# A three-layer float32 network on one core: SBUF laid out anew, operands of the split products at multiples of 256 bytes

## The chip, the core and the metric

The kernel runs on one NeuronCore of one Trainium2 chip. The metric is device time in microseconds of one execution, median of three runs. All arithmetic is float32; the large products run on TensorE in its `float32r` form.

## What is computed

A sequence of 256 tokens with 2048 features passes a first block (16 meta tokens are put ahead, so 272 tokens) and then a second block of two layers. Cut to the parts that carry the work:

```
h = concat(meta, x)                                   # block 1, 272 tokens
z = rmsnorm(h) @ w_in                                 # -> u, q_a, kv_a, k_pe
y = concat(rmsnorm(s5_mixer(u)), rmsnorm(mla_mixer(q_a, kv_a, k_pe)))
h = h + y @ w_out
h = h + (silu(conv3(gate)) * val) @ w_down            # gate, val = rmsnorm(h) @ w_up, 5504 each
x = rmsnorm(h)[16:]
for l in range(2):                                    # block 2, 256 tokens
    proj  = rms_norm(x) @ w_in[l]                     # four mixers of four heads, 128 wide
    mixed = concat(nsa, stick_breaking, forgetting, differential) @ w_out[l]
    x = x + rms_norm(mixed)
    x = x + rms_norm((gelu(conv3(gate)) * conv3(val)) @ mlp_w_down[l])   # 5632 each
```

## The kernel before

**Tiling.** Activations lie feature-major: a chunk is a tile of 128 features (partitions) by 256, 258 or 272 tokens. Each weight matrix streams through once, in half units of 128x1024 float32 (512 KB), loaded by SP's queue into `wraw` (five slots, names `wr`). `split` (line 532) turns each half unit into two quarters of 128x512: ScalarE writes the high part `wh`, VectorE the rest `wl = wr - wh`. Eight quarters are held in the pools `wh` and `wl`; in the feed-forward stages seven more pairs, `wxh` and `wxl`, come from `spare` (line 594). Activations are split in the same way (`split_act`, line 708) into `xh`/`xl` (16 chunks, pool `xp`), `yh`/`yl` (mixer outputs, pool `yp`) and `hhh`/`hhl` (the hidden layer of the feed-forward, five slots each, `hsplit`, line 1243).

**The split products.** Each product of a weight tile and an activation chunk is three matmuls into one PSUM bank, in `mm3`:

```
nc.tensor.matmul(acc, wh, xh, start=start, ...)   # line 626
nc.tensor.matmul(acc, wl, xh, start=False, ...)   # line 627
nc.tensor.matmul(acc, wh, xl, ..., stop=stop)     # line 628
```

The weight is the stationary operand (128 columns, 512 bytes in each partition), the activation streams as the moving operand: 256 columns are 1024 bytes in each partition. There are 8700 such triples. In `m2` the roles are exchanged: 512 columns of weights stream over stationary activations.

**The stages, in order of time** (us from the span's start): block 1's input projection, S5 mixer, latent attention and output projection, up to 430; its up product, 430 to 930 (43 pairs of a gate tile of 258 columns and a value tile of 256); its down product, 930 to 1165; then for each layer of block 2 projections and mixers (1180 to 1580, 2402 to 2840), up product (1580 to 2135, 2840 to 3357) and down product (2135 to 2387, 3357 to 3600). The last 20 us finish the norm and write out.

**What sets the order.** The program emits instructions one by one; a rough model of engine clocks (`_Model`) decides when the side work of a mixer or of an evacuation is emitted between matmuls. Nothing is reordered later. Pools are a stack: what is opened first lies lowest.

**Where operands begin.** A 16384-byte scratch for DMA descriptors lies at address 0, then four constants of 32 bytes each, then the pool `keep` with the residual `X`, then `xp` at 35424 (138 times 256, plus 96). A chunk slot is 272 float32, 1088 bytes, so each slot moves the start by 64 modulo 256: `xh` begins at 96 or 224, `xl` at 160 or 32. `wh`, `wl` and `wr` all begin at 96 modulo 256, `wxh` and `wxl` at 224. `hhh` and `hhl` lie behind the feed-forward's own tiles: at 32 modulo 256 in block 1, at 224 in block 2; `yh` and `yl` at 224 in block 2. Block 1's up product reads the gate from column 0 of `xh[k]` and the value from column 2 (line 1195), that is 8 bytes further.

Of the kernel before, what the change touches and what calls it, by code (L numbers as in the profile page):

```python
# [20 lines left out]
F32 = mybir.dt.float32  # L21
F32R = mybir.dt.float32r
# [7 lines left out]
D = 2048  # L30
L = 272      # tokens of block 1: 16 meta + 256
LQ = 258     # tokens 14..271: the ones whose output or conv input is needed
S = 256
CB = 16      # column of the residual tile where the 256 tokens begin
NP1 = 43     # gate/value pairs of block 1
# [4 lines left out]
# ---------------------------------------------------------------- layout on the host  # L40
# [49 lines left out]
CMP_AT = [14, 16, 18, 20, 22, 24, 25, 27, 28, 30, 31, 33, 34, 36, 37, 39]  # first products of the compression behind these halves  # L90
A_SEQ = [0, 3, 1, 2]  # mixers in the order of their projections: A, D, B, C
# [75 lines left out]
def _s5_consts():  # L167
    """Steps counted from the middle; which group each half of the partitions holds; which pair a group is in."""
    iota = np.broadcast_to(np.arange(L // 2) - 68.0, (128, L // 2))
    half = np.zeros((128, 128))  # L170
    pair = np.zeros((128, 32))
    g = np.arange(64)
    for p in range(128):
        half[g[g % 2 == p // 64], p] = 1
    pair[g, g // 2] = 1
    return np.concatenate([iota, half, pair], 1).astype(np.float32)
# [105 lines left out]
# ---------------------------------------------------------------- the kernel  # L282
# [4 lines left out]
class _Model:  # L287
    """A rough account of when each engine is through with what it was given; it only decides the order of emission."""
# [17 lines left out]
    def run(self, clk, eng, outs, ins, cost, done=60.0):  # L306
        """Returns the engine's clock after an instruction."""
        for ap in ins:
            for k in self.keys(ap):
                w = self.wr.get(k)  # L310
                if w is not None:
                    clk = max(clk, w[0] + (0.0 if w[1] == eng else 100.0))
        ok = [k for ap in outs for k in self.keys(ap)]
        for k in ok:
            for d in (self.rd, self.wr):
                w = d.get(k)
                if w is not None and w[1] != eng:
                    clk = max(clk, w[0] + 60.0)
        clk += cost
        for ap in ins:  # L320
            for k in self.keys(ap):
                self.rd[k] = (clk, eng)
        for k in ok:
            self.wr[k] = (clk + done, eng)
        return clk


class _Pool:
    """A tile pool; notes which slot a tile is in."""
# [12 lines left out]
class _Engine:  # L342
    """Passes calls on to an engine and keeps its clock."""
# [45 lines left out]
class Kern:  # L389
# [3 lines left out]
    def __init__(self, ctx, tc, A, out, parts, taps):  # L393
# [33 lines left out]
        self.raws, self.ready = {}, deque()  # L427
        p = self.keep = self.pool("keep")
        self.X = p.tile([128, 16, L], F32, name="X")
        self.xp = self.pool("xp")  # L430
        self.xh, self.xl = [None] * 16, [None] * 16
# [4 lines left out]
        self.wraw = self.pool("wraw", self.NRAW)  # L436
        self.wh = self.pool("wh", self.NQ)
        self.wl = self.pool("wl", self.NQ)
# [11 lines left out]
    def slot(self, name, c, dt=F32R):  # L450
        """A tile of one feature chunk in the slot name + c; what held the slot before is done with."""
        pool = self.xp if name[0] == "x" else self.yp
        return pool.tile([128, L], dt, name="%s%d" % (name, c))

# [8 lines left out]
    # ---- pacing  # L463
# [30 lines left out]
    def after(self, *engines, extra=150):  # L494
        """Absolute virtual time at which the engines have done what they were given."""
        return max([e.clk for e in engines]) + extra - self.t
# [17 lines left out]
    # ---- the stream of weights: loaded ahead, each quarter of a unit split into two 12 bit parts  # L514
# [45 lines left out]
    def release(self):  # L560
        """The uses of the quarters handed out last are out."""
        for x in self.used:
            if x is None:
                self.nfree += 1
            elif self.cap > self.NQ:
                self.extra.append(x)
        self.used = []
# [26 lines left out]
    def spare(self, st, n):  # L594
        """Room for n more quarters, split before the engines are busy with what a product waits for."""
        p = self.pool("wx", 1, st)
        self.extra = [tuple(p.tile([128, 512], F32R, name="wx%s%d" % (x, i)) for x in "hl") for i in range(n)]
        self.cap = self.NQ + n

    def unspare(self):  # L600
        """No further quarter goes there."""
        self.extra, self.cap = [], self.NQ

    def staged(self, n, *stages):
        """Runs the stages over n items, each a step behind the one before it."""
# [6 lines left out]
    def lead_in(self, gen, ahead):  # L612
        """The pre() of a product whose operands gen makes; weights split before carry the first steps."""
# [30 lines left out]
    def s4(self, b, ks, xs, n, pre=None, start=True, stop=True):  # L644
        """Four column tiles, outer loop over the chunks ks of the contraction."""
# [23 lines left out]
    def pair(self, accs, nk, xs, pre=None, tail=0, evac=None):  # L669
        """Two column tiles; a quarter holds two chunks of the contraction. The last tail quarters are taken together,  # L670
        one column tile after the other."""
# [24 lines left out]
    def m2(self, b, xh, xl, f, pre=None):  # L696
        """Token-major product: two tiles of 128 tokens against f columns."""
# [9 lines left out]
    # ---- norms  # L707
# [17 lines left out]
    def sumsq(self, count, n, eng):  # L725
        """Squares of count chunks: sq(c, src) squares one, add(c) adds it up; the last two stay apart."""
# [15 lines left out]
    def evacuate(self, dst, ps, gain, c, sq):  # L742
        """dst = gain * ps and the squares of ps, these first where they are waited for."""
# [6 lines left out]
    def turnaround(self, gen):  # L750
        """Statistics that everything waits for; the engines split weights meanwhile."""
# [5 lines left out]
    def presum(self, acc, n, bank):  # L757
        """The part of stats that belongs to the first of accs."""
# [4 lines left out]
    def stats(self, accs, n, nfeat, bank, rB, r_tok=None, wait=(), lock=False, pre=0):  # L763
        """rB[p, token] = rsqrt(sum of accs over partitions / nfeat + eps), on all partitions; r_tok the same by token."""
# [23 lines left out]
    def now(self, gen):  # L788
        """Emits a generator to its end at once."""
# [11 lines left out]
    # ================================================================ block 1  # L801
    def block1(self):
# [37 lines left out]
        # ---- input projection; the S5 mixer runs beside it  # L840
# [168 lines left out]
        # ---- q and k/v of the attention from their low-rank parts  # L1009
# [59 lines left out]
        # ---- the gate of the S5 mixer  # L1069
# [53 lines left out]
        # ---- latent attention beside the output projection of the S5 half  # L1123
# [27 lines left out]
        # ---- output projection of the attention half  # L1151
        parts, sqx, addx = self.sumsq(16, LQ, G)

        def evx(acc, t):
# [9 lines left out]
            for a in range(2):  # L1164
# [3 lines left out]
                self.split_act(a_[:, :LQ], b_[:, :LQ], xc, gn["ffn"][:, c:c + 1])  # L1168
# [14 lines left out]
        # ---- feed-forward  # L1183
        wx = ExitStack()
        self.spare(wx, 7)
        ff = ExitStack()
        fp = self.pool("f1", 1, ff)
# [7 lines left out]
        xf = lambda k, a: (self.xh[k][:, 2 * a:LQ], self.xl[k][:, 2 * a:LQ])  # L1195
# [37 lines left out]
    def conv(self, pool, u, w, name):  # L1233
        """Three taps over a tile that begins two tokens early."""
# [8 lines left out]
    def hsplit(self, pool, hh, k):  # L1243
        a = pool.tile([128, S], F32R, name="hhh", bufs=5)
        b = pool.tile([128, S], F32R, name="hhl", bufs=5)
# [3 lines left out]
    def down(self, pool, hh, n, last, q=None):  # L1249
        """All but the last four chunks of the down product, into all eight banks; last: the bank pair used before."""  # L1250
# [33 lines left out]
    def s5(self, sp, sp2, s5p, cc, u, ys, gn, state):  # L1284
        """The S5 mixer, two tokens to a step: S = lam B u[2j] + B u[2j+1], H[j] = lam^2 H[j-1] + S, y[2j+1] = C H[j],
        y[2j] = C lam H[j-1] + C B u[2j]. Each complex recurrence is a real one in the frame that turns with its state."""
# [263 lines left out]
    def mla(self, sp, cc, qn, qpe, kn, kpe, vv, yh, yl, accb, gain):  # L1550
# [10 lines left out]
        # meta queries of all heads at once, other heads' keys masked  # L1561
# [78 lines left out]
    # ================================================================ block 2  # L1640
    def layer(self, l, upd, wx, last):
# [7 lines left out]
        # x_new per chunk, its parts for the projection and its squares  # L1649
# [66 lines left out]
        # tiles of a mixer, once they are there; uses of each that are still to come  # L1716
# [7 lines left out]
        # ---- mixer A  # L1724
# [101 lines left out]
        # ---- output projection  # L1826
# [65 lines left out]
        # ---- feed-forward  # L1892
# [8 lines left out]
        ff = ExitStack()  # L1901
        fp = self.pool("f2", 1, ff)
# [84 lines left out]
    def rope(self, dst, src, n, kind):  # L1987
        """dst = src * cos + (R src) * sin, two tiles at a time; dst may be src."""
# [16 lines left out]
    def lock(self):  # L2005
        """Bank 7, for the side generators of block 1."""
# [3 lines left out]
    def take(self, n, m=0):  # L2010
        """Banks and head buffers, all at once."""
# [10 lines left out]
    def gates(self, E, vsw):  # L2022
        """Gates of mixer A and the running log forget of mixer C, from the token-major columns."""
# [19 lines left out]
    def compress(self, E, aux, ready):  # L2043
        """Compressed keys and values of mixer A."""
# [44 lines left out]
    def probs(self, bank, q, k, z, sm, scale, mul=None, bias=None):  # L2089
        """Causal softmax of one head (both query tiles) into z: queries on partitions."""  # L2090
# [24 lines left out]
    def turn(self, bank, z, pt, mask=None):  # L2115
        """Transposes z into pt: keys on partitions, [keys 0 x queries 0..255 | keys 1 x queries 128..255]."""
# [141 lines left out]
    def mix_b(self, E, M, need):  # L2258
# [3 lines left out]
        def heads(hs):  # L2262
# [10 lines left out]
            # what each key leaves and takes; the product of what the later keys leave  # L2273
# [141 lines left out]
```

## Time and profile before

| | |
|---|---|
| median of three runs | 3621.8 us (3620.7 to 3624.3) |
| span of the profiled execution | 3619.8 us |
| TensorE matmul busy | 3498.2 us, 97% |
| TensorE weight load busy | 3371.0 us, 93% |
| VectorE busy | 2427.3 us, 67% |
| ScalarE busy | 1715.0 us, 47% |
| GpSimd busy | 501.6 us, 14% |
| HBM read | 610.7 MB, 169 GB/s over the span |

The span is the time from the first to the last instruction of one execution; 2.0 us lie between it and the median. A matmul's record lasts some 280 ns, but the next one starts long before it ends, so the cost of a matmul in a dense stretch is read from the distance between starts, or from how many there are in 100 us.

### The profile page before, as it was taken

The numbers are of one execution on the slowest core, as the hardware profiler recorded it, in microseconds if no ns is written. First come the engines' busy times: TensorE is split into PE (matmuls) and PEld (weight loads), VectorE is DVE, ScalarE is ACT, GpSimd is POOL, SyncE is SP. The second block draws the span as 40 slices with busy tenths as digits, with TensorE's granted clock in tenths as the row PEclk, the third lists the DMA queues.
The fourth block names the chain that finished last, engine by engine and source line by source line (L and its number), as shares of the span: only waits on it lengthen the run. The fifth ranks groups of instructions, "written<-read, shape, count | busy, mean of one in ns | idle before, by whom it ended". The sixth has DMA issues, their size and how long they took to land. (4 is left out here: it accounts for less than half of the span.)

```text
span 3619.8 us, 70825 instructions
## 1 busy us (share of the span) xinstructions
PE 3498.2 (97%) x27995; PEld 3371.0 (93%) x27995; DVE 2427.3 (67%) x4592; ACT 1715.0 (47%) x3441; POOL 501.6 (14%) x547
## 2 busy tenths in 40 slices
PE   7879999999999999999999999999999999999997
PEld 7767999999999889899999999988889899999997
DVE  7896766666656656467777775565655777777654
ACT  5445544444555544454444444455445544444544
POOL 6652300000002100021000000030000300000002
PEclk9889999999999999999999999999999999999999
DMA  5323555555654644455555555536445455555553
GB/s 177 104 82 101 168 182 187 186 179 180 201 193 152 224 161 158 154 167 183 187 186 188 184 186 185 185 136 221 146 146 192 131 187 187 187 186 186 185 185 122
DMA packets 175022, 618.55 MB, mean 171 GB/s; under 512 B 20224, under 2 KB 24464, under 8 KB 174432
## 3 DMA queue, kind: packets, MB, share of 16 engines
q1 hardware_dynamic: 173488, 612.55, 51.0%
q8 instruction: 219, 3.59, 0.4%
q0 software_dynamic: 336, 0.77, 0.1%
q14 instruction: 115, 0.94, 0.1%
q10 hardware_dynamic: 864, 0.70, 0.1%
HBM read 610.72 MB, written 2.10 MB: 169 GB/s over the span
## 5 line engine op out<-in xcount | busy, mean ns | idle before, releaser
L379 DVE TENSOR_TENSOR wl<-wr,wh 128x512 fp32r<-128x512 f32 (+1 forms) x2000 | 1374.5, 714 | 826.7 <-ACT wh L379 823.4
L379 ACT ACTIVATE wh<-wr 128x512 fp32r<-128x512 f32 (+1 forms) x2014 | 1195.3, 623 | 898.3 <-PE ps L628 678.6
L628 PE MATMUL ps<-xl,wh 128*128 128x256 f32 (+2 forms) x4980 | 1420.2, 285 | 2.4 <-DVE xl L379 2.4
L626 PE MATMUL ps<-xh,wh 128*128 128x256 f32 (+2 forms) x4876 | 1395.6, 286 | 13.1 <-ACT xh L379 7.9
L627 PE MATMUL ps<-xh,wl 128*128 128x256 f32 (+2 forms) x4876 | 1389.4, 285 | 8.9 <-DVE wl L379 8.8
L626 PEld LDWEIGHTS ps<-xh,wh 128*128 128x128 f32 x4876 | 934.3, 192 | 26.7 <-issue 8.5
L628 PEld LDWEIGHTS ps<-xl,wh 128*128 128x128 f32 x4980 | 950.5, 191 | 3.6 <-DVE xl L379 3.5
L627 PEld LDWEIGHTS ps<-xh,wl 128*128 128x128 f32 x4876 | 932.8, 191 | 14.6 <-DVE wl L379 12.7
L626 PE MATMUL ps<-hhh,wh 128*128 128x256 f32 x1820 | 509.0, 280 | 2.3 <-ACT y L379 1.5
L628 PE MATMUL ps<-hhl,wh 128*128 128x256 f32 x1820 | 509.0, 280 | 0.1
L627 PE MATMUL ps<-hhh,wl 128*128 128x256 f32 x1820 | 508.0, 279 | 0.0
L626 PEld LDWEIGHTS ps<-hhh,wh 128*128 128x128 f32 x1820 | 342.4, 188 | 2.7 <-ACT y L379 1.7
L628 PEld LDWEIGHTS ps<-hhl,wh 128*128 128x128 f32 x1820 | 342.2, 188 | 0.3 <-DVE hhl L379 0.3
L627 PEld LDWEIGHTS ps<-hhh,wl 128*128 128x128 f32 x1820 | 342.2, 188 | 0.0
L379 POOL TENSOR_TENSOR acc<-acc,sq 128x256 f32<-128x256 f32 (+1 forms) x137 | 119.1, 869 | 1163.2 <-ACT sq L379 1158.2
L626 PE MATMUL ps<-yh,wh 128*128 128x258 f32 (+2 forms) x696 | 202.4, 291 | 12.8 <-DVE xl L379 8.6
L379 POOL TENSOR_TENSOR hh<-cv,cv 128x256 f32<-128x256 f32 x88 | 84.8, 964 | 896.4 <-DVE cv L379 855.3
L628 PE MATMUL ps<-yl,wh 128*128 128x258 f32 (+2 forms) x696 | 199.2, 286 | 2.0 <-DVE yl L379 2.0
L627 PE MATMUL ps<-yh,wl 128*128 128x258 f32 (+2 forms) x696 | 198.5, 285 | 0.0
L379 DVE SCALAR_TENSOR_TENSOR cv<-pad,cw,cv 128x256 f32<-128x256 f32 x352 | 180.6, 513 | 13.1
L628 PE MATMUL ps<-xl,wxh 128*128 128x256 f32 x588 | 167.5, 285 | 1.1 <-DVE xl L379 1.1
L379 DVE TENSOR_TENSOR wxl<-wr,wxh 128x512 fp32r<-128x512 f32 x230 | 162.3, 709 | 1.9 <-ACT wxh L379 1.9
(444 smaller groups left out, 4383.3 us busy)
## 6 DMA issues: line engine op xcount, KB each, us to landing
wr<-in_w_dram SPq DMA_DIRECT2D x1105, 512.0 KB, 4.6
wr<-in_cmpw_dram SPq DMA_DIRECT2D x32, 512.0 KB, 5.0
wr<-in_w_dram SPq DMA_DIRECT2D x16, 272.0 KB, 4.3
c2t<-in_c_dram SPq DMA_DIRECT2D x2, 1472.0 KB, 9.1
bc<-in_bc_dram SPq DMA_DIRECT2D x8, 256.0 KB, 3.6
X<-in_hT_dram SPq DMA_DIRECT2D x3, 544.0 KB, 10.0
out_dram<-X SPq DMA_DIRECT2D x5, 256.0 KB, 2.2
s5e<-yh SPq DMA_DIRECT2D x64, 17.0 KB, 2.1
```

The costliest lines, as they stand in the source:

```text
L379: return f(out, *a, **kw)
L626: nc.tensor.matmul(acc, wh, xh, start=start, stop=False, skip_group_check=True)
L627: nc.tensor.matmul(acc, wl, xh, start=False, stop=False, skip_group_check=True)
L628: nc.tensor.matmul(acc, wh, xl, start=False, stop=stop, skip_group_check=True)
```

## The change

The same instructions on the same data; what moves is where tiles lie in SBUF. The built programs have equal lists of instructions on TensorE and VectorE, in equal order, and on the other engines too but for a handful of waits (GpSimd two more and SP one fewer, ScalarE two more), which follow from tiles lying over other tiles than before. The scratch for DMA descriptors falls from 16384 to 4096 bytes; `pad0` (128 bytes) brings the next pool to 4352, 17 times 256; `xp`, `wh`, `wl` and `wraw` now come first, `keep` with the residual after them; a chunk slot is 320 float32, 1280 bytes, of which 272 are used; `hhh` and `hhl` get a pool of their own right behind `wx`. All of `wh`, `wl`, `wxh`, `wxl`, `wr`, `xh`, `xl`, `yh`, `yl`, `hhh`, `hhl` then begin at 0 modulo 256. In block 1's up product the chunks are now written and read at columns 14 to 271 of their slots, as elsewhere in block 1, so that the gate's moving operand begins 56 bytes behind such a multiple and the value's 64 bytes. Comments and docstrings are dropped. The diff, cut to its core:

```diff
+XW = 320
...
+        self.pool("pad0").tile([128, 32], F32, name="pad0")
+        self.xp = self.pool("xp")
+        self.xh, self.xl = [None] * 16, [None] * 16
+        self.wh = self.pool("wh", self.NQ)
+        self.wl = self.pool("wl", self.NQ)
+        self.wraw = self.pool("wraw", self.NRAW)
+        self.pool("pad1").tile([128, 40], F32, name="pad1")
         p = self.keep = self.pool("keep")
         self.X = p.tile([128, 16, L], F32, name="X")
-        self.xp = self.pool("xp")
-        self.xh, self.xl = [None] * 16, [None] * 16
...
-        self.wraw = self.pool("wraw", self.NRAW)
-        self.wh = self.pool("wh", self.NQ)
-        self.wl = self.pool("wl", self.NQ)
...
-        return pool.tile([128, L], dt, name="%s%d" % (name, c))
+        return pool.tile([128, XW], dt, name="%s%d" % (name, c))[:, 0:L]
...
-                self.split_act(a_[:, :LQ], b_[:, :LQ], xc, gn["ffn"][:, c:c + 1])
+                self.split_act(a_[:, 14:L], b_[:, 14:L], xc, gn["ffn"][:, c:c + 1])
...
+        self.hx = self.pool("hx1", 5, ff)
         fp = self.pool("f1", 1, ff)
...
-        xf = lambda k, a: (self.xh[k][:, 2 * a:LQ], self.xl[k][:, 2 * a:LQ])
+        xf = lambda k, a: (self.xh[k][:, 14 + 2 * a:L], self.xl[k][:, 14 + 2 * a:L])
...
-        a = pool.tile([128, S], F32R, name="hhh", bufs=5)
-        b = pool.tile([128, S], F32R, name="hhl", bufs=5)
+        a = self.hx.tile([128, S], F32R, name="hhh")
+        b = self.hx.tile([128, S], F32R, name="hhl")
...
+        self.hx = self.pool("hx2", 5, ff)
         fp = self.pool("f2", 1, ff)
...
-    nc = _bacc.Bacc("TRN2", target_bir_lowering=False, num_devices=1)
+    nc = _bacc.Bacc("TRN2", target_bir_lowering=False, num_devices=1, dynamic_dma_scratch_size=4096)
```

## Rows read from the trace of the kernel before

**Rows 1.** The page's parts 1 and 2: busy us by engine; granted clock, 40 slices.

```profile
PE 3498.2 (97%) x27995; PEld 3371.0 (93%) x27995; DVE 2427.3 (67%) x4592; ACT 1715.0 (47%) x3441; POOL 501.6 (14%) x547
...
PEclk9889999999999999999999999999999999999999
```

**Rows 2.** The view of waits, PE alone: us in total, times, longest us.

```profile
PE ps L507 <- DVE s5ab L379: 21.3, 6, 6.7
PE ps L512 <- POOL rtok L379: 12.4, 9, 3.0
PE ps L626 <- ACT xh L379: 9.4, 3, 6.0
```

**Rows 3.** Windows of 100 us, PE: length, busy (matmuls), granted clock, DMA share, GB/s.

```profile
950.00:1050.00 100.00, 100.00 (x885) 1.00 0.59 195
2170.00:2270.00 100.00, 100.00 (x844) 1.00 0.58 184
...
3400.00:3500.00 100.00, 100.00 (x845) 1.00 0.57 185
...
1700.00:1800.00 100.00, 100.00 (x846) 1.00 0.58 189
...
600.00:700.00 100.00, 100.00 (x832) 1.00 0.56 188
```

**Rows 4.** Timeline, PE, down products of block 1 and layer 0: start us, us.

```profile
1000.16 0.28 PE L628 MATMUL ps<-hhl,wh 128*128 128x256 f32 x1
...
1001.86 0.28 PE L628 MATMUL ps<-hhl,wh 128*128 128x256 f32 x1
...
2200.08 0.28 PE L628 MATMUL ps<-hhl,wh 128*128 128x256 f32 x1
...
2201.86 0.28 PE L628 MATMUL ps<-hhl,wh 128*128 128x256 f32 x1
```

**Rows 5.** Window of tile wh alone: PE, PEld, DVE, ACT, POOL busy (count).

```profile
2170.00:2270.00 100.00, 64.93 (x341) 53.83 (x339) 29.17 (x43) 27.18 (x43) 0.00 (x0) 1.00 0.58 184
```

**Rows 6.** Timeline, PE, short products; then tile hb: ns min/median/max of one.

```profile
1304.30 1.96 PE L507 MATMUL ps<-kcT,q 128*128 128x16 f32 x16 [0.27 <-DVE kcT L379]
1306.11 0.37 PE L626 MATMUL ps<-xh,wh 128*128 128x256 f32 x1
...
2726.14 0.82 PE L512 MATMUL ps<-ident,hb 128*128 128x128 f32 x6
...
L512 PE MATMUL ps<-ident,hb x136: 270/272/329, 1246.1 to 2728.7; 128*128 128x128 f32 x136
```

**Rows 7.** Groups of instructions by form, PE: count, busy us, mean ns, idle before.

```profile
L628 PE MATMUL ps<-xl,wh 128*128 128x256 f32 x4052 | 1148.4, 283 | 2.4 <-DVE xl L379 2.4
...
L626 PE MATMUL ps<-yh,wh 128*128 128x258 f32 x352 | 104.3, 296 | 11.8 <-DVE xl L379 7.6 <-ACT yh L379 4.0 <-DVE kpe L379 0.3
...
L626 PE MATMUL ps<-wh,xh 128*128 128x512 f32 x192 | 81.8, 426 | 0.0
...
L637 PE MATMUL ps<-xl,wh 128*128 128x256 f32 x16 | 4.4, 426 | 0.1
```

**Rows 8.** Timeline, PE, 512 columns of weights moving, layer 0: start us, us.

```profile
1417.40 0.39 PE L626 MATMUL ps<-wh,xh 128*128 128x512 f32 x1
...
1420.17 0.39 PE L626 MATMUL ps<-wh,xh 128*128 128x512 f32 x1
```

**Rows 9.** Windows by stage: length, busy of PE, PEld, DVE, ACT, POOL, clock, DMA.

```profile
0.00:310.00 310.00, 247.91 (x1907) 223.32 (x1907) 262.48 (x509) 153.38 (x355) 177.64 (x181) 0.91 0.38 125
310.00:430.00 120.00, 120.00 (x874) 105.93 (x873) 85.78 (x208) 64.82 (x152) 35.84 (x42) 1.00 0.39 129
...
1580.00:2135.00 555.00, 547.53 (x4559) 545.52 (x4559) 424.08 (x773) 253.91 (x474) 69.57 (x78) 0.99 0.55 179
```

**Rows 10.** The page's part 5: VectorE's rest of a quarter, by destination.

```profile
L379 DVE TENSOR_TENSOR wl<-wr,wh 128x512 fp32r<-128x512 f32 (+1 forms) x2000 | 1374.5, 714 | 826.7 <-ACT wh L379 823.4
...
L379 DVE TENSOR_TENSOR wxl<-wr,wxh 128x512 fp32r<-128x512 f32 x230 | 162.3, 709 | 1.9 <-ACT wxh L379 1.9
```

## Prediction

> **What bounds the kernel now.** [...] Busy does not say whether TensorE is held up, so the view of waits comes next: its longest waits are 21.3, 12.4 and 9.4 us in total [rows 2]. So the matmuls' own pace sets the end, and the question is what one costs. In stretches of 100 us in which TensorE never stops, with the clock at 1.00, there are 885 matmuls in block 1's down product, 844 to 846 in block 2's up and down products, 832 in block 1's up product [rows 3]: 113.0, 118.2 to 118.5, and 120.2 ns each. [...] The starts show the same: fifteen matmuls take 1.70 us in the one down product and 1.78 us in the other [rows 4], 113 and 119 ns.
>
> These two down products run the same code on tiles of the same size; every weight quarter of the first begins at 96 modulo 256, and the moving operand `hhh`/`hhl` at 32 there and at 224 in block 2. Is it the weights' place? In the window of layer 0, `wh` takes part in only 341 of 844 matmuls [rows 5] (two of each triple read it, so some 510 of 844 use these slots, and 330 the `wx` slots at 224); in the last layer, where no `wx` exists, all weights lie at 96, and the pace is the same (845) [rows 3]. So the moving operand's start is worth some 5 ns of 118, and the weights' start less than half a ns.
>
> **The change, part by part.** *Nothing is added, removed or reordered* on TensorE and VectorE; no queue is passed. Only places change, so the sum is counts times a change of pace.
>
> *The new pace* is not in the trace: no float32r matmul begins at 0 modulo 256. Lower bound: what a chain of other matmuls shows as the least distance for a load of 128 columns. Six transposes take 0.82 us, the last one 0.272, so (0.82 − 0.272)/5 = 110 ns; sixteen products with 16 columns, whose streaming is short, leave 1306.11 − 1304.30 = 1.81 us, 113 ns each, some first-start delay included [rows 6]. With the 10 ns steps of these rows, 108 to 113. [...] Upper bound of the likely: 113, the best pace seen, since operands that begin at 224 or 96 show that being off can cost more, and 0 is nearer to a whole number of pieces than 32 is. Upper bound in earnest: 118.5, no gain. I take 110, the transposes' row, as it has the same 128-column weight load and a stream that keeps up with it.
>
> (a) 256 moving columns. By form there are 25 groups, 21,408 matmuls, of which [rows 7] gives the first and the last. Block 1's up and down products have 43 × 16 × 3 = 2064 each of these, leaving 17,280 at 118.5 ns: 17,280 × 8.5 = 146.9 us.
>
> (b) Block 1's down product: 2064 × (113 − 110) = 6.2 us.
>
> (c) Block 1's up product: 2064 gates of 258 columns and 2064 values of 256, at 120.2. Their new starts, 56 and 64, are no multiples of 256. The gate stays 8 bytes off a multiple of 16, as the value is now: I give it nothing. The value gets a first piece of 192 bytes up to the next multiple of 256; between 32 (224 bytes, 113) and 224 (32 bytes, 118.5) I take 115: 2064 × 5.2 = 10.7 us. Ends: 0 for both, or 110 for both, 42 us.
>
> (d) 258 columns of `yh`/`yl`: three forms of 352 [rows 7]. Those before 310 us stand where VectorE is busy 262.5 of 310 us and TensorE 247.9 [rows 9]: VectorE's chain sets that stretch, so I count nothing. From 310 to 430 TensorE is never idle [rows 9]; two thirds of 1056 there, times 9 ns: 6 us.
>
> [...]
>
> Together 146.9 + 6.2 + 10.7 + 6 + 6.9 = 176.7 us.
>
> [...]
>
> *What is late next.* TensorE covers all the splitting and side work; with a shorter stream that cover shrinks. In layer 0's up product VectorE has 424 us in 555 [rows 9], 76%; shortened by 8.5/118.5 the stage is 515 and VectorE 82%: it keeps up. ScalarE's and VectorE's instructions get no cheaper: a `wl` at 96 takes 714 ns and a `wxl` at 224 takes 709 [rows 10]. In the mixers' stages chains of short steps (scores, softmax, transposes) end in TensorE, and what the stream gains there partly turns into waits. I take a tenth back, 17.7 us; ends: nothing and a fifth.
>
> *The smaller scratch and the new waits* on GpSimd, SP and ScalarE stand at the few loads of constants between stages; TensorE waits for GpSimd 12.4 us in all [rows 2]. Between −1 and +3 us; I take 0.
>
> Net 176.7 − 17.7 = 159.0 us. The span of 3619.8 becomes 3461; with the 2.0 us between span and median, 3621.8 − 159 = **3463 us**.
>
> **The rivals.**
>
> *Only as good as the best pace seen.* If 113 is the weight load's pace and not the stream's, (a) is 17,280 × 5.5 = 95 us, (b) is 0, (c) some 10, (d) and (e) half, 6: 111, less a tenth, 100 us; 3522 us. For it: the 113 ns of the short products; against it: the 110 of the transposes.
>
> [...]
>
> *The shorter stream becomes waits.* If the mixers' chains and VectorE take back half instead of a tenth, 177/2 = 88 us remain: 3534 us. For it, VectorE's 76%; against it, that the up product shows no wait of TensorE among the longest [rows 2].
>
> *All starts alike: slower.* After the change moving operand, next weight load and the splits' reads and writes all begin at 0 modulo 256. If the memory serves neighbours of equal start one after another, the pace becomes that of the worst stage now, 120.2: 17,280 × 1.7 + 2064 × 7.2 = 44 us more, 3666 us. It decides as soon as the mean pace is over 118.5. Against it: in layer 0's down product, `hhh` at 224 with `wx` at 224 is such a pair of equal starts already, and its window has 844 matmuls against 845 without any [rows 3, 5]; `wr`, `wh` and `wl` too share their start today.
>
> **How the numbers follow.** Forecast (pace 108 to 112) 0.65; best pace seen 0.16; no gain 0.07; half turned into waits 0.06; slower 0.06. The low end: 109 ns (another 17,280 + 2064 at 1 ns, 19 us), block 1's up product in full (31 more), nothing given back (18): 159 + 68 = 227, 3395 us. The high end: 113.3 ns, nothing in block 1's up product, half of (d) and (e), a fifth given back: (90 + 6) × 0.8 = 77, 3545 us. The rivals at 3522 and 3534 lie inside; some 0.18 stays outside. A measurement of this kernel tells some 0.2% from no change. Faster by more: 0.65 + 0.16 + 0.06 and a little of the rest, 0.87; within: 0.07; slower: 0.06.
>
> **What would show it.** Right: windows of 100 us in block 2's up and down products with some 905 matmuls instead of 845, block 1's down product at the same pace as block 2's (not above it as now), the 512-column starts 218 to 222 ns apart, and waits of TensorE up by some tens of us at most. Block 1's up product tells whether 64 or 256 is the unit: 832 grows to about 850 if only the value gains, to 900 if a multiple of 64 is enough. Wrong: 845 again (lines of 16), 885 everywhere (a weight load's pace), a pace near 110 with waits of 80 us and more (side work), or fewer than 840.

## The result, and the profile after

The change made the kernel slower, by 0.7%, which is more than the runs of either kernel spread. Its median is 3646.8 us (3641.4 to 3649.3, four runs) against 3623.1 (3620.7 to 3625.0, four runs) for the kernel before, a ratio of 1.0069 [1.0054, 1.0083]. The forecast was 3463 us. The profiled execution's span is 3644.3 us, 24.5 more than before.

The page of the changed kernel: first the busy us of each engine and the granted clock in 40 slices, as [rows 1]; then, from its table of groups, TensorE's third product of a triple and VectorE's rest of a quarter, as [rows 10] (lines 626 to 628 are now 630 to 632, line 379 is 380).

```profile
PE 3525.1 (97%) x27995; PEld 3400.4 (93%) x27995; DVE 2429.3 (67%) x4592; ACT 1714.4 (47%) x3441; POOL 502.2 (14%) x547
...
PEclk9889999999999999999999999999999999999999
...
L380 DVE TENSOR_TENSOR wl<-wr,wh 128x512 fp32r<-128x512 f32 (+1 forms) x2000 | 1375.3, 715 | 850.8 <-ACT wh L380 848.1
...
L632 PE MATMUL ps<-xl,wh 128*128 128x256 f32 (+2 forms) x4980 | 1417.1, 285 | 2.3 <-DVE xl L380 2.3
```

The counts of instructions, the clock, VectorE (715 ns a quarter for 714 before) and ScalarE (busy 1714.4 us for 1715.0) are as they were. TensorE alone is busy 27 us longer. Its waits did not grow; the view of waits, TensorE only (us in total, times, longest us), as [rows 2]:

```profile
PE ps L511 <- DVE s5ab L380: 20.4, 6, 5.7
PE ps L516 <- POOL rtok L380: 11.5, 9, 2.4
PE ps L630 <- ACT xh L380: 9.3, 3, 5.0
```

So the time went into the matmuls' own pace. Windows of 100 us in which TensorE never stops (length, busy us, matmuls, granted clock, DMA share, GB/s): block 1's up and down products, then up and down of layer 0 and up and down of layer 1. The same five stretches as [rows 3] are among them:

```profile
600.00:700.00 100.00, 100.00 (x845) 1.00 0.57 190
950.00:1050.00 100.00, 100.00 (x835) 1.00 0.55 183
1700.00:1800.00 100.00, 100.00 (x836) 1.00 0.56 180
2170.00:2270.00 100.00, 100.00 (x836) 1.00 0.59 185
2900.00:3000.00 100.00, 100.00 (x835) 1.00 0.56 191
3400.00:3500.00 100.00, 100.00 (x836) 1.00 0.57 184
```

Block 1's down product fell from 885 to 835 and block 2 from 844-846 to 836; block 1's up product, the one stage that the new layout leaves unaligned, rose from 832 to 845. The timeline of TensorE in layer 0's down product (start us, duration us), as [rows 4]:

```profile
2200.11 0.28 PE L630 MATMUL ps<-hhh,wh 128*128 128x256 f32 x1
2200.23 0.28 PE L631 MATMUL ps<-hhh,wl 128*128 128x256 f32 x1
2200.35 0.28 PE L632 MATMUL ps<-hhl,wh 128*128 128x256 f32 x1
...
2200.83 0.28 PE L630 MATMUL ps<-hhh,wxh 128*128 128x256 f32 x1
...
2201.91 0.28 PE L630 MATMUL ps<-hhh,wxh 128*128 128x256 f32 x1
```

Fifteen matmuls take 2201.91 − 2200.11 = 1.80 us: 120.0 ns each, and every single distance is 0.12 us, with `wh` and with `wxh` alike. 1.70 us in block 1's down product and 1.78 in this one stood there before. It is not the splits running beside it that hold TensorE up: between 2180 and 2350 us the mean distance is 120.0 ns for the 316 matmuls beside which neither VectorE nor ScalarE is busy, and 120.0 for the 1101 beside which one of them or both are.

Adding up the distances from one matmul's start to the next over the whole span, by kind, shows where the 25 us come from (to some 0.5 us, as it depends on which distances count as gaps). Matmuls of 256 columns: 2534.9 to 2561.4 us (+26.5). In these, the 2064 of block 1's down product give +13.7 (113.3 to 120.0 ns each), block 1's 2064 up values −5.9 (120.9 to 118.0), and the other 17,280 +18.7 (118.7 to 119.8). Matmuls of 258 columns give −1.7, of 512 −1.7 (230.3 to 227.4 ns each), the fp32 products −0.6, the longer gaps +2.8.

### The profile page after: what moved, and what is told of

The parts are those of the page before. It is cut to its first block, busy times and chain, and to the rows that moved or that the text cites. A ratio compares the mean times of both kernels' runs of the same rounds, so it can differ in the third digit from the quotient of the medians.

```text
span 3644.3 us, 70827 instructions
## 1 busy us (share of the span) xinstructions
PE 3525.1 (97%) x27995; PEld 3400.4 (93%) x27995; DVE 2429.3 (67%) x4592; ACT 1714.4 (47%) x3441; POOL 502.2 (14%) x547
## 4 chain that ended last, share of the span: by engine, by line
PE 51%; DVE 1%; POOL 1%; issue 1%; ACT 0%; DMA 0%; POOLq 0%; ACTq 0%; DVEq 0%
PE ps L630 17%; PE ps L631 16%; PE ps L632 16%; PE ps L511 2%; POOL acc L380 0%; DVE X L380 0%; PE ps L516 0%; DVE hb L380 0%; DVE y L380 0%; DVE wl L380 0%; DMA wr<-in_cmpw_dram 0%; DVE xh L380 0%; DVE xl L380 0%; POOL X L380 0%; ACT hb L380 0%
## 5 line engine op out<-in xcount | busy, mean ns | idle before, releaser
L380 POOL TENSOR_TENSOR acc<-acc,sq 128x256 f32<-128x256 f32 (+1 forms) x137 | 119.2, 870 | 1182.3 <-ACT sq L380 1178.9
```

Source lines behind the costliest of these rows:

```text
L380: return f(out, *a, **kw)
```

## The experiments

Every kernel is the changed one with the edit shown, save `e8_scratch`, which starts from the kernel before. "Triple" is the time of the three matmuls of a split product. Starts are always modulo 256 bytes, and "32 on 96" is a moving operand that begins at 32 with weights that begin at 96. Offsets in the diffs count elements of four bytes.

**All combinations at once.** Block 2's chunks get moving starts at every multiple of 16, and the weight slots starts at every multiple of 32.

```diff
+        o = 4 * c if self.shift and name[0] == "x" else 0
+        return pool.tile([128, XW], dt, name="%s%d" % (name, c))[:, o:min(o + L, XW)]
...
+            o = 8 * (self.nq % 8)
+            self.nq += 1
+            h = self.wh.tile([128, 576], F32R, name="wh")[:, o:o + 512]
+            l = self.wl.tile([128, 576], F32R, name="wl")[:, o:o + 512]
```

> The changed kernel with many starts at once. In block 2 the chunk k of xh and xl (k from 0 to 15) begins 16k bytes behind a multiple of 256, and the weight slots of wh and wl begin, in rotation, at 0, 32, 64 ... 224; wx stays at 0. Block 1 is as in the changed kernel. Theory M (the moving operand's start alone sets the pace): the distance of starts depends on k and not on the weight slot: 120 ns at k = 0, 113 at k = 2 (32 bytes), 118.5 at k = 14 (224 bytes). Theory C (moving operand and weights clash where their starts are equal): 120 ns for those pairs of chunk and slot whose starts agree modulo 256, and less, down to 113, for the others, at every k. [...]

One run took 3613.9 us against 3622.9 of the kernel before. The table takes block 2's runs of at least 12 successive matmuls with one pair of starts, called blocks here (the distances from the trace, the starts from the addresses in the built program). It leaves out a block's first two distances and its last, and gives the mean distance by the *difference*, moving start less weights' start, modulo 256:

```
difference  ns (blocks)      difference  ns (blocks)
   0       119.6 (138)         128      119.0  (95)
  16       114.6  (50)         144      118.6  (54)
  32       117.2  (96)         160      118.0  (93)
  48       118.2  (48)         176      119.3  (59)
  64       116.2  (87)         192      114.9 (100)
  80       119.1  (59)         208      119.0  (56)
  96       119.7 (100)         224      118.2  (96)
 112       117.5  (49)         240      117.1  (54)
```

Neither start alone explains this. With the moving operand at 0, weights at 0, 32, 64, 96, 128, 160, 192 and 224 give 119.6, 118.3, 116.3, 117.2, 119.7, 119.4, 116.1 and 117.7 ns. The difference does better: 0 on 0, 64 on 64 and 160 on 160 give 119.6, 119.5 and 119.3; 0 on 32, 96 on 128 and 224 on 0, all 224 apart, give 118.3, 118.1 and 118.3. Equal starts are nearly the worst, and starts 96 or 176 apart are as slow.

The differences 16, 64 and 192 have two paces each, and a block has one or the other: 192 runs at 113.6 in 65 blocks and at 117.5 in 35. Which one depends on what ran just before: all 28 blocks of 192 behind a chunk of difference 224 were slow, all 12 behind one of difference 0 were fast (28 of 28 and 11 of 12 in the finer map below). The 12, and 20 of the 28, are the same tile at the same pair of starts, `hhh` at 0 on 64. So something lasts beside the difference, perhaps how the two reads last fell into step; no row shows what it is.

**The same in steps of 4 bytes.**

```diff
-        o = 4 * c if self.shift and name[0] == "x" else 0
+        o = c if self.shift and name[0] == "x" else 0
```

> The map again with chunk k of xh and xl in block 2 beginning 4k bytes behind a multiple of 256 (k from 0 to 15), weight slots at 0, 32 ... 224 in rotation as in the first map, so that every multiple of 4 bytes appears as a difference. Theory C (the pace follows the difference of the two starts modulo 256): differences that both maps hold (0, 16, 32, 48 and their sums with 32) show the first map's paces (119.6 at 0, 114.6 at 16, 117.2 at 32, 114.9 at 192), whatever the two starts are alone. Theory M (the moving start alone): the pace goes by k. [...]

3620.4 us against 3623.2. At multiples of 16 most of the first map comes back (0: 119.6, 96: 119.5, 128: 119.6). The differences with two paces keep the paces and not the mean: 192 has 116.1, again from 113.4 and 117.8, and 64 has 117.7 for 116.2, as 65 of its 66 blocks run at the slower one. All weights begin at multiples of 32 here, so the rest modulo 16 is the moving operand's: starts at 0, 4, 8 and 12 past a multiple of 16 average 118.3, 120.5, 120.0 and 117.1 ns (586, 207, 219 and 222 blocks). No pair's mean in either pace lies below 113.3. So the place within 16 bytes matters too, by some 2 ns, though not as off or on a multiple alone: 12 past it is the quickest. The table within multiples of 16 has a spread of 5.

**One difference at a time.** `e2_w96` moves only the weights to 96, `e3_m32` only the moving operands to 32, `e4_m32_w96` both, which gives block 2's up products and layer 1's down product the pair that block 1's down product had in the kernel before.

```diff
+        self.pool("padw").tile([128, 24], F32, name="padw")
         self.wh = self.pool("wh", self.NQ)
...
-        self.pool("pad1").tile([128, 40], F32, name="pad1")
+        self.pool("pad1").tile([128, 16], F32, name="pad1")
...
+        p.tile([128, 24], F32, name="padx")
         self.extra = [tuple(p.tile([128, 512], F32R, name="wx%s%d" % (x, i)) for x in "hl") for i in range(n)]
```

> The changed kernel with the weights alone moved: wh, wl and wx begin at 96 modulo 256 instead of 0, the moving operands of the up products stay at 0. In the down products of block 1 and layer 0 the hidden layer slips to 96 as well, in layer 1 it stays at 0. Theory M: the up products of block 2 keep 833 matmuls in 100 us (120 ns); about 3647 us. Theory C: with unequal starts they rise to 850 to 885, the two down products with 96 on 96 stay at 833, layer 1's down product rises; 3560 to 3620 us.

```diff
-        return pool.tile([128, XW], dt, name="%s%d" % (name, c))[:, 0:L]
+        return pool.tile([128, XW], dt, name="%s%d" % (name, c))[:, 8:8 + L]
...
-        a = self.hx.tile([128, S], F32R, name="hhh")
+        a = self.hx.tile([128, XW], F32R, name="hhh")[:, 8:8 + S]
```

(and `hhl` like `hhh`).

> The changed kernel with the moving operands alone moved: xh, xl, hhh, hhl (and block 1's yh, yl) begin at 32 modulo 256, all weights stay at 0. Theory M: the pace of block 1's down product before, 113 ns, 885 matmuls in 100 us, in block 2's up products and in all down products; some 19,000 matmuls at 6.7 ns less: 127 us, 3520 us. Theory C: some pace below 120 as the starts differ, but 113 only by chance; 3520 to 3620 us.

> The changed kernel with both moved to the pair of block 1's down product before: moving operands at 32, weights at 96 modulo 256; in the down products of block 1 and layer 0 the hidden layer slips to 128. Theory M and theory C alike: 885 matmuls in 100 us in block 2's up products and in layer 1's down product, as that pair had before; 3520 to 3560 us. Where 128 on 96 comes out tells more: theory M says whatever the map shows for 128, theory C the pace that the map shows for a difference of 32. If neither pace appears, something else than these two starts set the 113 ns.

Against 3622.9 us of the kernel before: `e2_w96` 3621.8 (ratio 1.0001 [0.9989, 1.0013]), `e3_m32` 3599.1 (0.9932 [0.9916, 0.9949]), `e4_m32_w96` 3578.9 (0.9876 [0.9829, 0.9923]). Windows of `e2_w96`, TensorE, columns as above: block 1's down product, where `hhh` begins at 96 on 96, then the up products of layers 0 and 1, where the chunks begin at 0 on 96:

```profile
950.00:1050.00 100.00, 100.00 (x836) 1.00 0.56 182
1700.00:1800.00 100.00, 100.00 (x845) 1.00 0.56 181
...
2900.00:3000.00 100.00, 100.00 (x854) 1.00 0.52 178
```

Equal starts at 96 are as slow as equal starts at 0, 836 (a triple of exactly 360 ns), so a multiple of 256 has nothing to do with it; 0 on 96, difference 160, is 845 in one layer and 854 in the other. The weights' start, which the prediction priced at less than half a ns, is worth 9 to 18 matmuls in 100 us (the changed kernel has 836 and 835 there), and moving the weights alone takes back the 25 us that the change had lost. Windows of `e3_m32`, block 1's down and layer 1's up product:

```profile
950.00:1050.00 100.00, 100.00 (x859) 1.00 0.56 189
...
2900.00:3000.00 100.00, 100.00 (x852) 1.00 0.52 177
```

32 on 0 gives a triple of 350 ns in one stage and 353 in the other. Windows of `e4_m32_w96`, block 1's down product, then up and down of layer 0 and up of layer 1:

```profile
950.00:1050.00 100.00, 100.00 (x851) 1.00 0.55 185
1700.00:1800.00 100.00, 100.00 (x885) 1.00 0.61 202
2170.00:2270.00 100.00, 100.00 (x859) 1.00 0.59 189
2900.00:3000.00 100.00, 100.00 (x851) 1.00 0.53 181
```

Both up products run 32 on 96, difference 192; one is at the best pace seen, 340 ns a triple, the other at 353, and the four runs spread over 45 us around a median above the 3520 to 3560 us expected. So the two paces of one pair last for whole stages. In the two down products the hidden layer lies at 128 on 96 (in layer 0 for nine matmuls in ten): difference 32, and the triples take 353 and 350 ns, the two paces of 32 on 0 in `e3_m32`. That is the difference at work with both starts changed.

**Is it the load's length?** The second and third product load and compute 32 of the 128 weight columns.

```diff
+        m = min(32, acc.shape[0])
-        nc.tensor.matmul(acc, wl, xh, start=False, stop=False, skip_group_check=True)
-        nc.tensor.matmul(acc, wh, xl, start=False, stop=stop, skip_group_check=True)
+        nc.tensor.matmul(acc[:m], wl[:, :m], xh, start=False, stop=False, skip_group_check=True)
+        nc.tensor.matmul(acc[:m], wh[:, :m], xl, start=False, stop=stop, skip_group_check=True)
```

> The changed kernel with the second and third matmul of each triple cut to 32 of the 128 weight columns (so they add only to 32 rows of the output; the rest of the low parts is left out). The moving operands are read as before from 0 modulo 256, in full. A matmul streams while the weights of the next are loaded: the first and the second matmul of a triple then stream beside a load of 32 columns, the third beside one of 128. Theory C (the two reads disturb each other): the first two distances of a triple fall from 120 to about 108, the third stays between 113 and 120; 330 to 345 ns a triple instead of 360, some 890 matmuls in 100 us. Theory M (the moving read alone is slow from 0): all three stay at 120, 833 in 100 us.

3586.9 us, one run, against 3623.2. Groups by form, weight loads of the down products (count, busy us, mean ns), then the windows of layer 0's up and layer 1's down product:

```profile
L630 PEld LDWEIGHTS ps<-hhh,wh 128*128 128x128 f32 x1820 | 341.6, 188 | 19.3 <-ACT y L380 1.8 <-DVE X L380 1.1
L632 PEld LDWEIGHTS ps<-hhh,wl 128*32 128x32 f32 x1820 | 199.1, 109 | 0.0
```

```profile
1700.00:1800.00 100.00, 100.00 (x859) 1.00 0.59 193
...
3400.00:3500.00 100.00, 100.00 (x851) 1.00 0.56 188
```

A short load lasts 109 ns for the 188 of a full one, and the mean distance at difference 0 went from 120.0 ns to some 116.7 in block 1's down product and layer 0, and to 117.7 in layer 1. It did so in all three matmuls of a triple alike, within 1 ns, not in the two that stream beside a short load. So the pace of the stream depends on the loads around it, and theory M is out; that the load's reads hold up the stream's fits this but is not shown, as the cut matmuls also write fewer rows, and why the long load's neighbour gains as much as the others is open.

**Sixteen bytes apart.** Moving operands at 16, weights at 0.

```diff
+        return pool.tile([128, XW], dt, name="%s%d" % (name, c))[:, 4:4 + L]
...
+        a = self.hx.tile([128, XW], F32R, name="hhh")[:, 4:4 + S]
...
+        yh, yl = (yp.tile([128, 12 * S + 64], F32R, name=n)[:, 4:4 + 12 * S].rearrange("p (c n) -> p c n", c=12) for n in ("yh2", "yl2"))
```

> The changed kernel with every moving activation 16 bytes behind a multiple of 256 (xh, xl, yh, yl, hhh, hhl) and every weight at such a multiple. In block 1's up product gate and value then begin at 72 and 80. Theory C with the first map (16: 113.3 ns in 36 of 50 places): 885 matmuls in 100 us in block 2's up and down products and in block 1's down product; 3647 less some 20,000 times 6.5 ns, so about 3515 to 3535 us, and steadier over the rounds than the pair 32 on 96. Theory M: the pace of k = 1 in the first map, 118; 3610 us.

3591.0 us, ratio 0.9913 [0.9891, 0.9935]. Windows: block 1's down, layer 0's down and layer 1's down product:

```profile
950.00:1050.00 100.00, 100.00 (x885) 1.00 0.56 195
...
2170.00:2270.00 100.00, 100.00 (x845) 1.00 0.56 186
...
3400.00:3500.00 100.00, 100.00 (x860) 1.00 0.56 188
```

The same code with the same starts has three paces here: triples of some 340, 355 and 350 ns. The expectation, 885 in all of these stages and 3515 to 3535 us, was missed: the difference alone does not tell the pace.

**The scratch alone**, in the kernel before:

```diff
-    nc = _bacc.Bacc("TRN2", target_bir_lowering=False, num_devices=1)
+    nc = _bacc.Bacc("TRN2", target_bir_lowering=False, num_devices=1, dynamic_dma_scratch_size=4096)
```

> The kernel before with one part of the change alone: the scratch for DMA descriptors is 4096 instead of 16384 bytes; all else moves down by 12288 bytes, 48 times 256, so all starts modulo 256 stay. Theories C and M alike: no change, 3619 to 3626 us. If the smaller scratch held up loads, some us more.

3621.7 us, ratio 0.9996 [0.9986, 1.0005]: it costs and brings nothing.

**The best difference everywhere, and a push into the 340 ns pace.** Moving operands at 192, weights at 0; in `e9_kick` chunk 0 and every eleventh `hhh`/`hhl` begin at 0, because blocks of difference 192 behind one of difference 0 were fast. `e10_d192` is the same without these.

```diff
+        o = 0 if c == 0 and name[0] == "x" and self.xo == 48 else self.xo
+        return pool.tile([128, XW], dt, name="%s%d" % (name, c))[:, o:o + L]
...
+        o = 48 if self.nh % 11 else 0
+        self.nh += 1
+        a = self.hx.tile([128, XW], F32R, name="hhh")[:, o:o + S]
...
+        yh, yl = (yp.tile([128, 12 * S + 64], F32R, name=n)[:, 48:48 + 12 * S].rearrange("p (c n) -> p c n", c=12) for n in ("yh2", "yl2"))
```

(`self.xo` is 48 elements, 192 bytes, and 32 while block 1's up chunks are written.)

> Theory C with states: the pace of a pair of starts depends on their difference and on how the two reads fell into step; 192 has a state of 113.3 and one of 117.8 ns, which lasts, and the first map shows which one is entered: behind a chunk of difference 0 the fast one (20 of 21 in both maps), behind one of 224 the slow one. The changed kernel with moving activations at 192 and weights at 0, but the chunk 0 of xh and xl and every eleventh chunk of the hidden layer at 0, so that the step is set anew at the price of one chunk at 120. In block 1's up product gate and value begin at 184 and 192. Expected: 880 matmuls in 100 us in all up and down products of block 2 and in block 1's down product, some 860 in block 1's up product; 3647 - 102 - 13 - 9 = about 3523 us, within 10 us from run to run. Without states (the difference alone decides): a mean of the two, 115 to 116, 3560 us.

> The same without the chunks at 0: every moving activation at 192, all weights at 0. Theory C with states: whole stages at 113.3 and others at 117.8, by chance, so times that differ by tens of us from run to run, like the pair 32 on 96 (3555 to 3600 us). Without states: one pace everywhere, and times as close to each other as those of the kernel before.

`e9_kick` took 3537.1 us (3535.5 to 3540.1, four runs), ratio 0.9765 [0.9753, 0.9778], 14 us more than expected; `e10_d192` 3536.7 (3524.5 to 3560.3, six runs), ratio 0.9781 [0.9752, 0.981], mostly quicker than expected. Both beat both kernels by more than 80 us. Windows of `e9_kick`, all six stages:

```profile
600.00:700.00 100.00, 100.00 (x843) 1.00 0.56 185
950.00:1050.00 100.00, 100.00 (x879) 1.00 0.57 191
1700.00:1800.00 100.00, 100.00 (x882) 1.00 0.57 189
2170.00:2270.00 100.00, 100.00 (x882) 1.00 0.59 193
2900.00:3000.00 100.00, 100.00 (x881) 1.00 0.53 182
3400.00:3500.00 100.00, 98.52 (x864) 1.00 0.58 185
```

Its chunks at 192 have a median triple of 340 ns in every stage of block 2 and in block 1's down product, those at 0 354 to 360. Without the push the profiled run has 884 or 885 in these stages where TensorE never stops, but the runs differ by 36 us instead of 5. Four and six runs are few; that the push holds the 340 ns pace is likely by this, and not settled. It costs what it gains: the medians are equal. Block 1's up product (gate at 184, value at 192) stays at 843, where 860 was expected: its gates take a mean of 364.5 ns a triple, and the values behind them 348.8 in place of 340.

**What is 113.3 the pace of?** From `e10_d192`, once with short loads (the edit of `e6_short_load`) and once with short streams, where the second and third matmul of a triple stream 192 of 256 columns beside full loads:

```diff
+        c = n * 3 // 8 * 2
-        nc.tensor.matmul(acc, wl, xh, start=False, stop=False, skip_group_check=True)
-        nc.tensor.matmul(acc, wh, xl, start=False, stop=stop, skip_group_check=True)
+        nc.tensor.matmul(acc[:, :c], wl, xh[:, :c], start=False, stop=False, skip_group_check=True)
+        nc.tensor.matmul(acc[:, :c], wh, xl[:, :c], start=False, stop=stop, skip_group_check=True)
```

> The kernel with all moving activations at 192 and all weights at 0, and the second and third matmul of each triple cut to 32 weight columns (the rest of the low parts is left out). The first two matmuls of a triple then stream beside a short load. If 113.3 ns is the pace of a full weight load, those two distances fall to about 109 and the triple to some 332 ns (905 matmuls in 100 us). If it is the pace of the stream itself, 340 stays (885), or more if the short load brings another step between the two reads: with both at 0 the triple went from 360 to 350 to 353 with short loads, not to 336.

> [...]

3520.9 and 3485.4 us, one run each, against 3628.8 of the kernel before. Window of `e11_short_load192`, layer 0's up product, and then the timeline of TensorE's matmuls and weight loads of `e12_short_stream` in block 1's down product (start us, duration us):

```profile
1700.00:1800.00 100.00, 100.00 (x884) 1.00 0.62 202
```

```profile
999.94 0.30 PE L632 MATMUL ps<-hhh,wh 128*128 128x256 f32 x1
999.96 0.19 PEld L634 LDWEIGHTS ps<-hhh,wl 128*128 128x128 f32 x1
1000.08 0.25 PE L634 MATMUL ps<-hhh,wl 128*128 128x192 f32 x1
1000.09 0.19 PEld L635 LDWEIGHTS ps<-hhl,wh 128*128 128x128 f32 x1
1000.17 0.27 PE L635 MATMUL ps<-hhl,wh 128*128 128x192 f32 x1
1000.19 0.19 PEld L632 LDWEIGHTS ps<-hhh,wh 128*128 128x128 f32 x1
1000.28 0.30 PE L632 MATMUL ps<-hhh,wh 128*128 128x256 f32 x1
1000.30 0.19 PEld L634 LDWEIGHTS ps<-hhh,wl 128*128 128x128 f32 x1
```

With two of three loads a quarter as wide a triple still takes 340 ns, in three equal steps, so the length of the load is not what holds the stream of 256 columns at 113.3. With two of three streams a quarter shorter the triple also takes 1000.28 − 999.94 = 0.34 us, but not in equal steps: the loads, all of 128 columns, start 0.13, 0.10 and 0.11 us apart (122, 108 and 110 ns in the unrounded trace), the longest step behind the full stream. So a full load can follow the one before after 108 to 110 ns, and 113.3 is not the load's own pace. What holds this triple at 340 ns is not shown, nor what makes 113.3 the least for 256 columns: no run shortened loads and streams together. No pair of starts in the two maps ran below 113.3. In the one stage that does not run at this pace, block 1's up product, the two kernels have 867 and 881 matmuls in 100 us against 843; the rest of what they gained was not followed up.

## Why the prediction was wrong

**The step that failed** is "so the moving operand's start is worth some 5 ns of 118, and the weights' start less than half a ns". It came from a comparison inside one stage: layer 0's down product runs `hhh` at 224 half on `wh` at 96 and half on `wx` at 224, and its pace equals that of the last layer, which has only 96 [rows 3, 5]. With the addresses laid beside the trace of before, the two pairs measure 119.1 (68 blocks of six matmuls or more, difference 128) and 119.3 ns (65 blocks, difference 0). The map has 119.0 and 119.6 for these differences at other starts: two slow pairs that happen to be equally slow. Block 1's down product, 32 on 96, is difference 192, one of the two best of the table, at the quicker of its two paces: 113.3 ns from start to start, before as in the experiments. (The 113.0 of the prediction divides 100 us by a count that takes in the matmuls running over both edges of the window; the other paces by counts are low by as much.) The reading "starts at 32 are good" should have been "32 on 96 is good"; the weights' start was tried at two places for one moving start, where the map has eight: with the moving operand at 0 they range from 116.1 to 119.7 ns.

**The new pace of 110**, the second step that failed, extrapolated from one trait (nearness to a multiple of 256) past the best pace seen. Aligning all operands gave difference 0 nearly everywhere: 120.0 ns in the steady stages, where the old layout had a mix. In block 2's up products before, chunks at 32, 96, 160 and 224 rotate over weights at 96 and 224, which gives the differences 192, 0, 64 and 128. Their pace, 118.2 in layer 0 [rows 3], lies among the map's means for these four, 114.9 to 119.6, but the map does not give it matmul by matmul: in layer 1's up product, on weights at 96, triples with `xh` at 96 and `xl` at 160 take 352 ns and those with 224 and 32 take 363, where the map would have 355 and 353 to 356. What a change of start inside a triple does was not tried. Nor did any stream of 256 columns run at 110: 113.3 was the least mean of any stretch in any run. The rows that the 110 was taken from, six transposes, stream 128 columns for each load; they tell the least distance of two loads, which `e12_short_stream` has at 108 to 110 too, and bound no stream of 256.

**The terms.** (a) 146.9 us gained became 18.7 lost. (b) 6.2 gained became 13.7 lost, the largest loss per matmul, since it had the best pair. (c) came near by luck: block 1's up values gained 5.9 us for 10.7, its gates, to which (c) gave nothing, some 2.4 (120.3 to 119.2 ns), and 832 became 845, near the 850 that the prediction had for "only the value gains". Its reason, a first piece up to the next multiple of 256, no run shows; in the map 64 on 0 is one of the better pairs by its difference (116.2 on average). (d) lost some 0.5 us for a gain of 6: the `yh`/`yl` products from 310 to 430 us went from 119.9 to 120.7 ns, and the 1.7 us gained with 258 columns are the gates'. (e), the 512 columns: no run shows the 6.9 us nor starts 218 to 222 ns apart; the runs gave 1.7 us, 230.3 to 227.4 ns. Half of the 6.9 is in the rival at 3522 us and in the high end too.

**The rivals.** "All starts alike: slower", at 0.06, is what happened, with equal starts slow and nearly its pace, 120.2 for 120.0. Its reason, neighbours of equal start served one after another, is not shown: 96 apart is as slow. Its 44 us came out as 25 because the 17,280 had been at 118.7 and ended at 119.8 on average, and because block 1's up product and the 512 columns gained. What spoke against it in the prediction was the comparison above. "No gain", at 0.07, with 845 again, did not come: block 2 has 835 or 836. The place within 16 bytes shows in `e5_map_fine`: starts 4 and 8 past a multiple of 16 cost some 2 ns (120.5 and 120.0 for 118.3), a start 12 past is 1.2 ns quicker (117.1), and the larger part of the map's spread, 114.6 to 119.7, lies between starts that are all multiples of 16. "Only as good as the best pace seen" had the right floor, 113, for the wrong layout and by luck, as its condition, 113 as the weight load's pace, does not hold (108 to 110): `e10_d192` reaches the floor, with 3537 us near the 3522 that this rival gave.

**What was right.** TensorE's pace sets the end. Nothing else became late, as the waits after show against [rows 2]. VectorE's and ScalarE's instructions cost the same at other starts (a `wl` 715 ns for 714, a `wh` 622 for 623), and the smaller scratch is free (ratio 0.9996). The point named as proof of the opposite, "fewer than 840", is what the windows showed.

**What stays open.** Why the pace goes by the difference at all, and why the unit is 256 bytes; what makes a pair of starts take up or leave its quicker pace (a chunk of difference 224 before it makes 192 slow, one of 0 makes it fast, in nearly all blocks, but no cause is shown); why a short load speeds up all three matmuls of a triple; what makes 113.3 ns the least; and a good pair for block 1's up product, whose gates and values lie 8 bytes apart, so that one of them is always off a multiple of 16: the best seen with all its work was 851 in 100 us, in `e7_d16`.

## What to carry to other kernels

Where TensorE streams one operand while it loads the next (in `e12_short_stream` a load starts 0.01 to 0.02 us behind the start of a matmul whose record lasts 0.25 to 0.30), ask for the starts of both, not for round addresses: here equal starts were among the worst, and one pair's difference is worth 6 ns of 118 on every matmul. Before an operand's start is called worth nothing, try more than two of its places: two slow pairs look like "no effect". Where the same code at the same addresses shows two paces, look at many runs: the best one is not the time of the layout.

## What was unexpected of the hardware

- The pace of split products depends on the distance of moving and stationary operand modulo 256 bytes: 113.3 to 120.0 ns for 256 columns with starts at multiples of 16, at a granted clock of 1.00. The weights take part in it: the pace changes from 119.6 to 116.1 when their start alone goes from 0 to 192, and from 120.0 to some 117 when two of three loads are shorter.
- The same pair of starts runs at two or three paces that last for a whole stage: triples of 340 and 353 ns at 32 on 96, of 340, 350 and 355 at 16 on 0.
- In long stretches equal starts run at exactly 120.0 ns for 256 columns, and 113.3 is the least mean of any stretch. Loads of 128 columns follow one another at 108 to 110 ns behind the short streams of `e12_short_stream`.
